# Up-projection of a gated FFN by seven products, with the hidden rows through DRAM

## The chip, the cores and the metric

The kernel runs on one core of a Trainium2 chip. The metric is device time in microseconds (us) of one execution; lower is better. The core has TensorE (PE, with its weight loads PEld), VectorE (DVE), ScalarE (ACT), GpSimd (POOL) and SyncE (SP, which issues most DMAs).

## The reference

One layer of a decoder step for 1024 prompt tokens and 8 x 4 sample tokens (T = 1056 columns in all, D = 1024 features). Latent attention and a state-space branch are merged and projected by w_out; then a gated FFN with a causal width-3 convolution on its up-projection, and an embedding gate, follow. The part that the change touches, in float32:

```python
x = x + mixed @ lw['w_out']
up = rmsnorm(x, lw['g_ffn']) @ lw['w_up']              # 1024 -> 2 x 2816
full = jnp.concatenate([buf, up], axis=1)              # two rows of history in front
conv = lw['conv_b'] + full[:, 0:s] * lw['conv_w'][0]   # + taps 1 and 2
a, v = jnp.split(conv, 2, axis=-1)
x = x + (jax.nn.gelu(a) * v) @ lw['w_down']            # 2816 -> 1024
x = x + jax.nn.sigmoid(rmsnorm(x, lw['g_ple']) @ lw['w_ple_gate']) * (p @ lw['w_ple_proj'])
```

The outputs also include the last rows of the up-projection.

## The kernel before

Features lie on partitions (128 at a time) and tokens on columns. To keep float32 accuracy each operand of a matmul is split into a high part, rounded to float32r by a cast on ACT, and a low part, the rest, by a subtraction on DVE or GpSimd (split, L79). mm3 (L83) then makes three matmuls for each product: high by high, high by low, low by high. The tokens are cut into three blocks of BLK = 352 columns.

The program is written in order and the tile framework places instructions on each engine's queue and adds the semaphores; each engine works its queue in order. Tiles of one tag share a number of buffers (bufs), and a writer waits until the last reader of its buffer is done.

*w_out.* For each of 8 output chunks o, 3 blocks x 8 k x 3 matmuls accumulate in PSUM (tile pm). DVE adds them to the residual x2, which stays in SBUF for all tokens; hi_lo and squares make the operands gh and gl2 of the up-projection and the sums of squares. The norm's factor of each token (rms_sums, rsqrt at L93, rms_rows) is not in the operands: it is multiplied in when the up-projection leaves PSUM (scaled_).

*FFN.* There are 22 hidden blocks of 128 rows (NH), each with a gate half a and a value half v, so 44 up-halves (up_half, L1690). An up-half makes 24 products of 352 columns, which scaled_ takes out of PSUM (L1712). conv (L1721) makes the convolution: a first term on ACT, two taps on DVE with two SBUF operands each (L1726; L1728 for the sample tokens). Then Gelu on ACT, the product of the halves and its split on DVE. The weights of an up-half (up_w, wload) come by one DMA of 512 KB, a cast on ACT and a subtraction on GpSimd (L81). After two hidden blocks down() (L1778) multiplies them with their rows of w_down: for each block and each output chunk two hidden blocks are added up in PSUM, and DVE adds the result to x2 (L1787). The last down() also prepares the operands of the embedding gate.

*Embedding gate.* For each of 8 output chunks and each block: 24 matmuls with w_ple_gate (gate), 6 with w_ple_proj (rest), the sigmoid on ACT, the sum, turned back by TensorE and written out (out_turn).

The order around it is the plain order of the program text: up-halves run one after another, down() of two hidden blocks is traced between two up-halves, and `last_rows` sends out the up-projection's last rows at the end.

## Time and profile before

| | |
|---|---|
| median of 3 runs | 2093.94 us (2093.68 to 2095.9) |
| span of the profiled execution | 2091.9 us |
| PE busy | 2004.0 us (96%), 12558 matmuls |
| PEld busy | 1888.6 us (90%) |
| DVE busy | 1154.0 us (55%) |
| ACT busy | 741.4 us (35%) |
| POOL busy | 552.8 us (26%) |
| granted TensorE clock, mean | 0.974 |
| DMA | 134.58 MB, mean 64 GB/s |

The profiled execution's own time is its span, from the first to the last instruction; the runs' median lies 2.0 us above it. Busy times of PE are of pipelined matmuls, whose recorded durations overlap; the distance of their starts tells their pace. Idle time of an engine that is not the bottleneck costs nothing.

### The profile page before, as it was taken

The page shows a single profiled execution, that of the slowest core. Times are in us where ns is not written, and L with a number is a line of the kernel's source. Part 1 is how long each engine was busy: PE and PEld are TensorE (multiplying, and loading weights), DVE is VectorE, ACT ScalarE, POOL GpSimd, SP SyncE. Part 2 cuts the span into 40 slices and gives each one's busy share as a digit, 9 for nine tenths or more (in the row PEclk, how much of TensorE's full clock was granted, in tenths as well). Part 3 has the DMA queues.
Part 4 walks back from the last instruction along what each step waited for, and adds up shares of the span by engine and source line. Part 5 has one row for each costly group of instructions (what it writes and reads, how often), then busy time and mean ns, then how long its engine had stood idle before and what let it go on. Part 6 is the DMA issues. An engine that isn't in the chain of part 4 may idle for free.

```text
span 2091.9 us, 32712 instructions
## 1 busy us (share of the span) xinstructions
PE 2004.0 (96%) x12558; PEld 1888.6 (90%) x12558; DVE 1154.0 (55%) x2481; ACT 741.4 (35%) x1499; POOL 552.8 (26%) x679
## 2 busy tenths in 40 slices
PE   7998999999998799999999999999999999999999
PEld 6997888888786688889999999999999999999898
DVE  6517532245878856665655555555545554556612
ACT  5522332343665545444333312222221222124422
POOL 1106341111223312223431412222222222214432
PEclk9999999999999979999999999999999999999999
DMA  7402222243321000004441211111111111111121
GB/s 247 125 18 59 61 68 63 66 142 106 91 61 40 28 12 1 2 26 155 129 154 42 71 41 51 51 41 37 56 44 48 31 61 41 51 31 55 45 73 52
DMA packets 175942, 134.58 MB, mean 64 GB/s; under 512 B 34577, under 2 KB 162500, under 8 KB 175786
## 3 DMA queue, kind: packets, MB, share of 16 engines
q1 hardware_dynamic: 168874, 123.84, 19.8%
q10 hardware_dynamic: 6912, 8.65, 1.2%
q8 instruction: 99, 1.62, 0.3%
q14 instruction: 57, 0.47, 0.1%
HBM read 104.87 MB, written 26.24 MB: 63 GB/s over the span
## 4 chain that ended last, share of the span: by engine, by line
PE 80%; DVE 10%; ACT 4%; issue 2%; DMA 2%; POOL 1%; SPq 0%; ACTq 0%; DVEq 0%; POOLq 0%
PE pu L85 9%; PE pu L84 9%; PE pu L86 9%; PE pm L85 5%; PE pm L86 5%; PE pm L84 5%; PE pd L84 4%; PE pd L86 3%; PE pd L85 3%; PE pt L84 3%; PE pt L86 2%; PE pt L85 2%; PE pv L1372 2%; PE p L84 2%; PE p L86 1%
## 5 line engine op out<-in xcount | busy, mean ns | idle before, releaser
L84 PE MATMUL pu<-gh,wh 128*128 128x352 f32 x1248 | 404.8, 324 | 0.0
L86 PE MATMUL pu<-gh,wl 128*128 128x352 f32 x1248 | 404.6, 324 | 0.0
L85 PE MATMUL pu<-gl,wh 128*128 128x352 f32 x1248 | 403.9, 324 | 0.0
L86 PEld LDWEIGHTS pu<-gh,wl 128*128 128x128 f32 x1248 | 235.8, 189 | 0.0
L84 PEld LDWEIGHTS pu<-gh,wh 128*128 128x128 f32 x1248 | 235.7, 189 | 0.1
L85 PEld LDWEIGHTS pu<-gl,wh 128*128 128x128 f32 x1248 | 235.5, 189 | 0.1
L81 POOL TENSOR_TENSOR wl<-ws,wh 128x1024 fp32r<-128x1024 f32 x68 | 167.4, 2462 | 132.3 <-ACT wh L80 126.8
L1726 DVE SCALAR_TENSOR_TENSOR cv<-up,cw,cv 128x1024 f32<-128x1024 f32 (+2 forms) x92 | 157.0, 1707 | 58.2 <-ACT cv L1722 58.1
L1787 DVE TENSOR_TENSOR x<-pd,x 128x352 f32<-128x352 f32 x264 | 135.9, 522 | 92.2 <-PE pd L86 92.2
L84 PE MATMUL pd<-hh,dwh 128*128 128x352 f32 x528 | 172.6, 327 | 7.6 <-DVE x L1787 7.6
L85 PE MATMUL pd<-hl,dwh 128*128 128x352 f32 x528 | 170.4, 323 | 0.0
L86 PE MATMUL pd<-hh,dwl 128*128 128x352 f32 x528 | 170.4, 323 | 0.0
L1712 DVE TENSOR_TENSOR up<-pu,t 128x352 f32<-128x352 f32 x132 | 66.9, 509 | 162.6 <-PE pu L86 162.6
L80 ACT CAST wh<-ws 128x1024 fp32r<-128x1024 f32 x68 | 71.4, 1050 | 168.0 <-PE pu L85 149.5
L86 PE MATMUL pm<-xh,wl 128*128 128x352 f32 x384 | 127.8, 333 | 0.0
L85 PE MATMUL pm<-xl,wh 128*128 128x352 f32 x384 | 127.1, 331 | 0.0
L84 PE MATMUL pm<-xh,wh 128*128 128x352 f32 x384 | 126.8, 330 | 0.0
L84 PEld LDWEIGHTS pd<-hh,dwh 128*128 128x128 f32 x528 | 99.3, 188 | 12.3 <-DVE x L1787 12.3
L85 PEld LDWEIGHTS pd<-hl,dwh 128*128 128x128 f32 x528 | 99.6, 189 | 0.1
L86 PEld LDWEIGHTS pd<-hh,dwl 128*128 128x128 f32 x528 | 99.4, 188 | 0.0
L1372 PEld LDWEIGHTS pv<-Vt,Pt 128*128 128x128 f32 x576 | 78.8, 201 | 3.7 <-ACT Pt L1358 0.5
L1372 PE MATMUL pv<-Vt,Pt 128*128 128x65 f32 x576 | 78.3, 278 | 0.1
(705 smaller groups left out, 4728.5 us busy)
## 6 DMA issues: line engine op xcount, KB each, us to landing
ws<-w_up SPq DMA_DIRECT2D x44, 512.0 KB
wst<-w_in SPq DMA_DIRECT2D x16, 512.0 KB
cb<-cache_ckv SPq DMA_DIRECT2D x64, 128.0 KB
dga<-go ACTq DMA_DIRECT2D x24, 176.0 KB
dgs<-go ACTq DMA_DIRECT2D x24, 176.0 KB
ga<-dga SPq DMA_DIRECT2D x8, 528.0 KB
gs<-dgs SPq DMA_DIRECT2D x8, 528.0 KB
x<-dxt SPq DMA_DIRECT2D x8, 528.0 KB
```

Source lines behind the costliest of these rows:

```text
L80: A.copy(hi, src)
L81: (eng or G).tensor_tensor(lo, src, hi.bitcast(F32), OP.subtract)
L84: PE.matmul(out, lh, rh, start=start, stop=False)
L85: PE.matmul(out, lh, rl, start=False, stop=False)
L86: PE.matmul(out, ll, rh, start=False, stop=stop_)
L1372: PE.matmul(W["pv"][:, j, :DV + 1], Pts[k][:, q0:q0 + 128], Vb[hp][:, k, e], start=k == 0, stop=k == i)
L1712: V.tensor_tensor(U[:, 2 + n * BLK:2 + n * BLK + w], pu[n][:, :w], rbc[:, n * BLK:n * BLK + w], OP.mult)
L1726: V.scalar_tensor_tensor(C[:, c0:c1], U[:, c0 + tp:c1 + tp], w[tp], C[:, c0:c1], op0=OP.mult, op1=OP.add)
L1787: V.tensor_tensor(x2[:, o, c], pd, x2[:, o, c], OP.add)
```

## The change

The up-projection of a hidden block is seen as a 2 x 2 by 2 x 2 block product. The weights' blocks are the two halves of the 1024 features by the two halves a and v; the operand's blocks are the two halves of the features by two quarters (QW = 264 columns) of a token half (HW = 528). Strassen's scheme in Winograd's form makes it with seven products instead of eight. Each product has 4 k x 3 matmuls of 264 columns. The sums of weight blocks and of operand blocks that it needs are made before the split into high and low parts (wprod, operands), the sums of products in PSUM or when they leave it (up_pair). The norm's factor now goes into the operands (scale).

The order of hidden blocks is `occ`: hidden blocks 0 to 3 for the first token half alone, 4 to 21 for both halves, and 0 to 3 again for the second half; so wprod runs 26 times. Weight parts are made three products ahead (ahead). Operands of the second token half are made in steps between the products of the first four (todo), the gate half's convolution, Gelu and the product of the halves in steps of the next occurrence (post).

w_out is made by token halves in blocks of 264 columns, with its weights loaded and split once per half; the residual goes to DRAM (dx2). The merge, which makes w_out's operands, writes them in quarters (mx).

The hidden rows are no longer split and multiplied at once. They go to DRAM (dhid). After all of the up-projection three token blocks (384, 384, 288 columns) are worked one after another (block): hidden rows of the block are loaded and split (hid_in, hid_out), w_down is multiplied with all 22 hidden blocks added up in PSUM, and then the block's embedding gate follows. w_down, w_ple_gate and w_ple_proj are loaded and split once per block (wunit: units of up to 4 x 128 rows, the cast on ACT and the subtraction on GpSimd). The next block's hidden rows are loaded and split during the gate.

```diff
+HW = T // 2
+QW = T // 4
...
-        mh = pm.tile([128, 8, T], F32R, name="mh")
-        ml = pm.tile([128, 8, T], F32R, name="ml")
+        mx = [[[x_tile(pm, 16) for _ in "hl"] for _ in range(2)] for _ in range(4)]
...
+        NJ = 4
+        occ = [(j, 0, 1) for j in range(NJ)] + [(j, 0, 2) for j in range(NJ, NH)] + [(j, 1, 1) for j in range(NJ)]
+        ORDER = (1, 6, 2, 7, 5, 4, 3)
+        def raw_tile():
+            return praw.tile([128, 8, 128], F32, name="raw", tag="raw", bufs=5)
+        raws = {}
...
+        wsum = {}
+        def wprod(i, m):
+            a, v = raws[i]
+            a1, a2, v1, v2 = a[:, 0:4], a[:, 4:8], v[:, 0:4], v[:, 4:8]
+            if m == 6:
+                s = wsum[i] = wp.tile([128, 2, 4, 128], F32, name="wsum", tag="ws", bufs=1)
+                G.tensor_tensor(s[:, 0], v1, v2, OP.add)
+                G.tensor_tensor(s[:, 1], s[:, 0], a1, OP.subtract)
+            if m == 7:
+                G.tensor_tensor(v1, a1, v1, OP.subtract)
+            if m == 3:
+                G.tensor_tensor(a2, a2, wsum[i][:, 1], OP.subtract)
+            s = {1: a1, 2: a2, 4: v2, 7: v1, 3: a2}.get(m)
+            if s is None:
+                s = wsum[i][:, 0 if m == 5 else 1]
+            w = wp.tile([128, 2, 4, 128], F32R, name="wx", tag="w", bufs=4)
+            A.copy(w[:, 0], s)
+            (G if m in (2, 5, 4) else V).tensor_tensor(w[:, 1], s, w[:, 0].bitcast(F32), OP.subtract)
+            if m == ORDER[-1]:
+                load_raw(i + 2)
+            return w
+        wseq = [lambda i=i, m=m: wprod(i, m) for i in range(len(occ)) for m in ORDER]
+        wq = []
+        def ahead(n):
+            while wseq and len(wq) < n:
+                wq.append(wseq.pop(0)())
...
+        def wo_evac(h, o, p_):
+            x = XP[h, o % 4][:, o // 4]
+            x_q = x.rearrange("p (n c) -> p n c", n=2)
+            V.tensor_tensor(x_q, p_[:, :, :QW], x_q, OP.add)
+            SP.dma_start(dx2[o * 128:(o + 1) * 128, h * HW:(h + 1) * HW], x)
             if o == 0:
-                A.activation(sqs[:, c], x2[:, o, c], AF.Square, scale=1.0 / 32.0)
+                A.activation(sqs, x, AF.Square, scale=1.0 / 32.0)
             else:
-                A.activation(sq, x2[:, o, c], AF.Square, scale=1.0 / 32.0)
-                eng.tensor_tensor(sqs[:, c], sqs[:, c], sq, OP.add)
...
+            def hl(m, k, src, eng):
+                hi, lo = (x[:, k] for x in tile_of(m))
+                A.copy(hi, src)
+                eng.tensor_tensor(lo, src, hi.bitcast(F32), OP.subtract)
+            def scale(k):
+                for g in range(2):
+                    x = XP[h, k][:, g]
+                    V.scalar_tensor_tensor(x, x, gcol["g_ffn"][:, 4 * g + k:4 * g + k + 1], rbh, op0=OP.mult, op1=OP.mult)
+            def first(k):
+                b11, b12, b21, b22 = (XP[h, k][:, g, q * QW:(q + 1) * QW] for g in range(2) for q in range(2))
+                hl(1, k, b11, V)
+                hl(2, k, b21, G)
+                hl(3, k, b22, V)
+                V.tensor_tensor(b11, b12, b11, OP.subtract)
+                G.tensor_tensor(b12, b22, b12, OP.subtract)
+            def second(k):
+                t1, t3, b21, b22 = (XP[h, k][:, g, q * QW:(q + 1) * QW] for g in range(2) for q in range(2))
+                V.tensor_tensor(b22, b22, t1, OP.subtract)
+                hl(6, k, b22, V)
+                hl(7, k, t3, G)
+                hl(5, k, t1, V)
+                G.tensor_tensor(b21, b21, b22, OP.subtract)
+                hl(4, k, b21, V)
+            return ([lambda k=k: scale(k) for k in range(4)] + [lambda k=k: first(k) for k in range(4)] +
+                    [lambda k=k: second(k) for k in range(4)])
+        for h in range(2):
+            for o in range(8):
+                wh, wl = W.pop(0)
+                if o < 7:
+                    W.append(wload((w_out[:, :, (o + 1) * 128:(o + 2) * 128], 0, 8)))
+                elif h == 0:
+                    W.append(wload((w_out[:, :, 0:128], 0, 8)))
+                else:
+                    ahead(2)
+                p_ = psq_.tile([128, 2, 512], F32, name="q")
+                for n in range(2):
+                    for k in range(8):
+                        mh, ml = mx[2 * h + n][k // 4]
+                        mm3(p_[:, n, :QW], wh[:, k], wl[:, k], mh[:, k % 4], ml[:, k % 4], k == 0, k == 7)
+                if h and o == 0:
+                    rst = half_sums()
+                wo_evac(h, o, p_)
+                if h == 0 and o < 4:
+                    x_load(1, o)
+                if h == 0 and o == 7:
+                    todo = operands(0)
+                if h and o == 1:
+                    half_rows(rst)
+                if h and o > 1:
+                    for _ in range(2):
+                        todo.pop(0)()
+                if h and o in (3, 5):
+                    load_raw((o - 3) // 2)
...
+            def prods(m, t, start):
+                w = wq.pop(0)
+                ahead(3)
+                for n in range(ng):
+                    xh_, xl_ = XT[g0 + n][m]
+                    for k in range(4):
+                        o_ = t[:, n, :QW]
+                        for x, (l_, r_) in enumerate(((w[:, 0, k], xh_[:, k]), (w[:, 0, k], xl_[:, k]), (w[:, 1, k], xh_[:, k]))):
+                            PE.matmul(o_, l_, r_, start=start and k + x == 0, stop=k + x == 5, skip_group_check=not start)
...
+            P = acc()
+            prods(1, P, True)
+            v = P[:, :ng, :QW]
+            A.copy(part(1, 0), v)
+            step()
+            Q = acc()
+            prods(6, Q, True)
+            V.tensor_tensor(part(0, 1), Q[:, :ng, :QW], part(1, 0), OP.add)
+            step()
+            prods(2, P, False)
+            A.copy(part(0, 0), v)
+            step()
+            prods(7, Q, False)
+            V.tensor_tensor(part(1, 1), Q[:, :ng, :QW], part(1, 0), OP.add)
+            step()
+            R = acc()
+            prods(5, R, True)
+            V.tensor_tensor(part(1, 1), R[:, :ng, :QW], part(1, 1), OP.add)
+            step()
+            prods(4, Q, False)
+            V.tensor_tensor(part(1, 0), Q[:, :ng, :QW], part(1, 0), OP.add)
...
+            conv(1)
+            prods(3, R, False)
+            V.tensor_tensor(part(0, 1), R[:, :ng, :QW], part(0, 1), OP.add)
+            def hidden():
+                V.tensor_tensor(Cs[0][:, :tot], Cs[0][:, :tot], Cs[1][:, :tot], OP.mult)
+                SP.dma_start(dhid[j * 128:(j + 1) * 128, g0 * HW:g0 * HW + tot], Cs[0][:, :tot])
+            post.append(lambda: conv(0))
+            post.append(lambda: A.activation(Cs[0][:, :tot], Cs[0][:, :tot], AF.Gelu_apprx_tanh))
+            post.append(hidden)
...
+        def hid_split(b, r, t, eng):
+            pool, n_ = (hid1, 16) if r < 8 else (p2, 6)
+            w = TB[b][1]
+            hi, lo = (pool.tile([128, 2, 384], F32R, name="hd", tag="hd", bufs=n_)[:, :, :w] for _ in "hl")
+            split(t, hi, lo, eng)
+            hp_[r] = hi, lo
+        def wunit(x):
+            kind, b, o, kg = units[x]
+            t = unit_raw(units[x])
+            if x + 2 < len(units):
+                unit_raw(units[x + 2])
+            n = 2 if (kind == "d" and kg == 5) or (kind == "g" and kg == 2) else 4
+            s = t[:, 4 * (kg % 2):4 * (kg % 2) + n]
+            w = wp.tile([128, 2, 4, 128], F32R, name="wx", tag="w", bufs=4)
+            split(s, w[:, 0, :n], w[:, 1, :n])
+            return w
+        wseq += [lambda x=x: wunit(x) for x in range(len(units))]
...
+            def down_group(pd, kg):
+                wt = wq.pop(0)
+                ahead(3)
+                for k in range(4 * kg, min(4 * kg + 4, NH)):
+                    hi, lo = (x[:, k % 2] for x in hp_[k // 2])
+                    mm3(pd, wt[:, 0, k % 4], wt[:, 1, k % 4], hi, lo, k == 0, k == NH - 1)
+            def down_out(o, pd):
+                V.tensor_tensor(xb[o], pd, xb[o], OP.add)
+                gg = GG[o] = pA.tile([128, 2, HW + 4], F32R, name="gg", tag="A", bufs=8)[:, :, :w]
+                g = gcol["g_ple"][:, o:o + 1]
+                A.activation(gg[:, 0], xb[o], AF.Copy, scale=g)
+                V.scalar_tensor_tensor(gg[:, 1], xb[o], g, gg[:, 0].bitcast(F32), op0=OP.mult, op1=OP.subtract)
+                if o == 0:
+                    A.activation(sqb, xb[o], AF.Square, scale=1.0 / 32.0)
+                else:
+                    sq = p2.tile([128, 384], F32, name="sq", bufs=2)[:, :w]
+                    A.activation(sq, xb[o], AF.Square, scale=1.0 / 32.0)
+                    (V if o == 7 else G).tensor_tensor(sqb, sqb, sq, OP.add)
...
+            nxt = list(range(NP_)) if b < 2 else []
+            for o in range(8):
+                pg_ = gate(o)
+                if o == 0:
+                    rst = sums()
+                pp_ = proj(o)
+                if o == 0:
+                    rows(rst)
+                rest(o, pg_, pp_)
+                if o:
+                    out_turn(o - 1)
+                for r in list(hraw):
+                    hid_out(*r)
+                for r in nxt[:2]:
+                    hid_in(b + 1, r)
+                nxt = nxt[2:]
```

## Rows read from the trace of the kernel before

**Rows 1.** Windows: us; busy PE, PEld, DVE, ACT, POOL (instructions); clock, DMA share, GB/s.

```profile
1068.70:1161.00 92.30, 92.30 (x580) 92.30 (x578) 49.28 (x70) 30.62 (x56) 19.56 (x8) 1.00 0.28 93
1162.00:1948.00 786.00, 777.11 (x4807) 770.28 (x4807) 443.46 (x705) 207.14 (x257) 206.39 (x260) 1.00 0.15 47
1948.00:2091.90 143.90, 135.74 (x847) 131.35 (x845) 42.64 (x82) 37.10 (x71) 39.34 (x32) 0.96 0.21 61
```

**Rows 2.** Timeline of TensorE: first matmul of a down() call, start and duration.

```profile
1299.69 0.43 PE L84 MATMUL pd<-hh,dwh 128*128 128x352 f32 x1 [0.58 <-DVE x L1787]
```

**Rows 3.** Timeline of TensorE: dense runs of 384, 288, 256 columns, first and last.

```profile
56.20 0.34 PE L84 MATMUL pm<-wah,xh 128*128 128x384 f32 x1
...
60.22 0.34 PE L86 MATMUL pm<-wah,xl 128*128 128x384 f32 x1
60.40 0.30 PE L84 MATMUL pm<-wah,xh 128*128 128x288 f32 x1
...
63.44 0.30 PE L86 MATMUL pm<-wah,xl 128*128 128x288 f32 x1
...
594.09 0.28 PE L85 MATMUL pt<-wkl,ch 128*128 128x256 f32 x1
...
594.57 0.28 PE L86 MATMUL pt<-wkh,cl__5571 128*128 128x256 f32 x1
```

**Rows 4.** Groups of GpSimd by shape: count, busy us and mean ns, idle before.

```profile
L81 POOL TENSOR_TENSOR wl<-ws,wh 128x1024 fp32r<-128x1024 f32 x57 | 138.2, 2424 | 108.4 <-ACT wh L80 102.9
...
L1896 POOL TENSOR_TENSOR y<-y,x 128x352 f32<-128x352 f32 x21 | 19.7, 942 | 47.5 <-DVE y L1895 47.5
...
L81 POOL TENSOR_TENSOR wkl<-kst,wkh 128x512 fp32r<-128x512 f32 x4 | 5.1, 1279 | 1.0 <-ACT wkh L80 1.0
```

**Rows 5.** Groups of DVE by shape, same columns.

```profile
L1787 DVE TENSOR_TENSOR x<-pd,x 128x352 f32<-128x352 f32 x264 | 135.9, 522 | 92.2 <-PE pd L86 92.2
...
L1759 DVE TENSOR_TENSOR cv<-cv 128x1056 f32<-128x1056 f32 x21 | 26.1, 1242 | 0.0
...
L81 DVE TENSOR_TENSOR wal<-wast,wah 128x512 fp32r<-128x512 f32 x4 | 2.8, 688 | 0.4 <-ACT wah L80 0.4
...
L1726 DVE SCALAR_TENSOR_TENSOR cv<-up,cw,cv 128x352 f32<-128x352 f32 x4 | 2.3, 585 | 1.5 <-ACT cv L1722 1.4
```

**Rows 6.** Timelines of DVE and GpSimd at three places of the FFN.

```profile
1181.82 1.27 DVE L1726 SCALAR_TENSOR_TENSOR cv<-up,cw,cv 128x1024 f32<-128x1024 f32 x1
1181.91 3.44 POOL L81 TENSOR_TENSOR wl<-ws,wh 128x1024 fp32r<-128x1024 f32 x1
...
1223.65 2.41 POOL L81 TENSOR_TENSOR wl<-ws,wh 128x1024 fp32r<-128x1024 f32 x1
1224.57 0.53 DVE L1787 TENSOR_TENSOR x<-pd,x 128x352 f32<-128x352 f32 x1 [0.44 <-PE pd L86]
...
1259.26 2.41 POOL L81 TENSOR_TENSOR wl<-ws,wh 128x1024 fp32r<-128x1024 f32 x1
1260.43 2.32 DVE L1726 SCALAR_TENSOR_TENSOR cv<-up,cw,cv 128x1024 f32<-128x1024 f32 x1 [1.59 <-ACT cv L1722]
1262.67 0.24 DVE L1728 SCALAR_TENSOR_TENSOR cv<-up,cw,cv 128x32 f32<-128x32 f32 x1
1262.84 1.27 DVE L1726 SCALAR_TENSOR_TENSOR cv<-up,cw,cv 128x1024 f32<-128x1024 f32 x1
```

**Rows 7.** Groups of ACT by shape, same columns.

```profile
L1722 ACT ACTIVATE cv<-up,cw 128x1024 f32<-128x1024 f32 x43 | 53.2, 1238 | 0.0
...
L80 ACT CAST wah<-wast 128x512 fp32r<-128x512 f32 x8 | 5.0, 624 | 0.8 <-DMA wast<-w_in 0.8
```

**Rows 8.** Timeline of DVE: first and last step of an inverse root.

```profile
1166.88 0.17 DVE L1651 TENSOR_SCALAR msx<-pt 128x8 f32<-128x8 f32 x1 [1.22 <-PE pt L1647]
...
1169.19 0.17 DVE L111 SCALAR_TENSOR_TENSOR rst<-rf_a,rf_i 128x9 f32<-128x9 f32 x1
```

**Rows 9.** The page's 40 equal slices: what DMA moved.

```profile
GB/s 247 125 18 59 61 68 63 66 142 106 91 61 40 28 12 1 2 26 155 129 154 42 71 41 51 51 41 37 56 44 48 31 61 41 51 31 55 45 73 52
```

More of the change, by code (lines that the diff above doesn't have):

```diff
@@ L1614, in body @@
         mo.close()
[L1617 to L1624 removed]
+        praw = ctx.enter_context(tpool(name="praw", bufs=1, side="right"))
@@ new lines, in body, with operands, tile_of @@
+        XT = {}
+        def operands(h):
+            pool, n_ = (px, 12) if h == 0 else (pm, 16)
+            X = XT[h] = {}
+            def tile_of(m):
+                if m not in X:
+                    p_, b_ = (px, 12) if h == 0 and len(X) < 6 else (pm, 16)
+                    X[m] = x_tile(p_, b_), x_tile(p_, b_)
+                return X[m]
+            def hl(m, k, src, eng):
+                hi, lo = (x[:, k] for x in tile_of(m))
+                A.copy(hi, src)
+                eng.tensor_tensor(lo, src, hi.bitcast(F32), OP.subtract)
+            def scale(k):
+                for g in range(2):
+                    x = XP[h, k][:, g]
[17 more added lines that the diff above has]
+                    [lambda k=k: second(k) for k in range(4)])
@@ new lines, in body @@
+        todo = []
+        for k in range(4):
+            x_load(0, k)
+        for h in range(2):
[26 more added lines that the diff above has]
+                    load_raw((o - 3) // 2)
@@ new lines, in body @@
+        R2 = {}
+        todo = [lambda: R2.update(r=half_sums()), lambda: half_rows(R2["r"])] + operands(1)
+        for i in range(NH):
+            up_pair(i)
+            if i == NJ - 1:
+                assert not todo
+        pX.close()
+        TB = ((0, 384), (384, 384), (768, 288))
+        NP_ = NH // 2
+        w_dn = I["w_down"].rearrange("o (k p) n -> p (o k) n", p=128)
+        w_pp = I["w_ple_proj"].rearrange("o (k p) n -> p (o k) n", p=128)
+        dhv = dhid.rearrange("(k p) t -> p k t", p=128)
@@ new lines, in body, with unit_raw @@
+        units = []
+        for b in range(3):
+            units += [("d", b, o, kg) for o in range(8) for kg in range(6)]
+            units += [("g", b, o, kg) for o in range(8) for kg in range(3)]
+        rawq, wraw = {}, [0]
+        def unit_raw(u):
+            kind, b, o, kg = u
+            key = kind, b, o, kg // 2
+            if key not in rawq:
+                t = rawq[key] = raw_tile()
+                oc = slice(o * 128, (o + 1) * 128)
+                if kind == "d":
+                    k0, k1 = 8 * (kg // 2), min(8 * (kg // 2) + 8, NH)
+                    SP.dma_start(t[:, :k1 - k0], w_dn[:, k0:k1, oc])
+                elif kg < 2:
+                    SP.dma_start(t, w_pg[:, :, oc])
+                else:
+                    SP.dma_start(t[:, :2], w_pp[:, :, oc])
+            return rawq[key]
@@ new lines, in body, with hid_in, hid_out, none @@
+        hraw = {}
+        def hid_in(b, r):
+            hraw[b, r] = hid_load(b, r)
+        def hid_out(b, r):
+            hid_split(b, r, hraw.pop((b, r)), V)
+        def none():
+            pass
+        for r in range(0, 8, 2):
+            todo += [lambda r=r: hid_in(0, r), none, lambda r=r: (hid_out(0, r), hid_in(0, r + 1)), none,
+                     lambda r=r: hid_out(0, r + 1)]
+        for i in range(NH, len(occ)):
+            up_pair(i)
+        while post:
+            step()
@@ L1806, in last_rows @@
                 PE.transpose(pt[:18, j * 128:(j + 1) * 128], LU[:, q + j], ident)
-            lo_ = pn2.tile([18, 512], F32, name="lo_", bufs=LOB)
+            lo_ = p2.tile([18, 512], F32, name="lo_", bufs=1)
             A.copy(lo_, pt[:18])
-            SP.dma_start(cvp[:, q * 128:(q + 4) * 128], lo_[0:2])
-            SP.dma_start(cvs[:, q * 128:(q + 4) * 128], lo_[2:18])
-        ready = [q for q in range(0, NH2, 4) if max(order.index(q + i) for i in range(4)) < NH2 - 2]
-        for q in ready:
-            last_rows(q)
+            A.dma_start(cvp[:, q * 128:(q + 4) * 128], lo_[0:2])
@@ L1830, in p_turn @@
+        def p_turn(b):
+            w, ld = TB[b][1], pld.pop(b)
+            pT[b] = [p2.tile([128, 2, 384], F32R, name="pT" + x, bufs=1) for x in "hl"]
             for k in range(2):
                 pt = ps.tile([128, 512], F32, name="pt")
-                for j in range(nj):
-                    PE.transpose(pt[:, j * 128:j * 128 + n], ld[:n, j, k * 128:(k + 1) * 128], ident[:n, :n])
-                c, w = slice(j0 * 128, j0 * 128 + nj * n), nj * n
-                A.copy(pTh[k][:, c], pt[:, :w])
@@ L1836, in p_turn @@
-                V.tensor_tensor(pTl[k][:, c], pt[:, :w], pTh[k][:, c].bitcast(F32), OP.subtract)
-        sqs3 = pn2.tile([128, T], F32, name="sqs3", tag="hl", bufs=3)
-        def after(o, c):
-            hi_lo(o, c, gcol["g_ple"][:, o:o + 1])
-            squares(o, c, sqs3, pn2.tile([128, S + 2 + NB * 6], F32, name="sq3", tag="up")[:, :BLK], G)
-        down((NH - 2, NH - 1), after)
-        for n in range(3):
-            p_turn(n)
-        w_pp = I["w_ple_proj"].rearrange("o k n -> (o k) n")
@@ L1919, in host_consts @@
+        for r in range(8, NP_):
+            hid_in(0, r)
+        for r in range(8, NP_):
+            hid_out(0, r)
+        for b in range(3):
+            block(b)
 def host_consts():
```

429 lines of the change are left out of this document (209 added, 220 removed).

## The prediction

> **What bounds the kernel now.** I read the work by stage first. From the w_out projection on, TensorE is busy nearly throughout: the projection 92.3 of 92.3 us, the FFN 777 of 786, the gate stage 136 of 144 [rows 1]. VectorE (DVE) is at 56% of the FFN and GpSimd (POOL) at 26%. So the time is TensorE's, and a change gains what it takes off TensorE and loses what it makes TensorE wait. One regular wait exists already: TensorE sits 0.58 us before the first matmul of each of the ten inner down() calls [rows 2].
>
> The pace of matmuls comes next, since a recorded duration overlaps its neighbours and only starts tell it. The projection's 576 products of 352 columns fill 92.3 us: 0.1602 us each [rows 1]. Of 384 columns, 24 start in 56.20 to 60.22, 0.1748 each; of 288, 24 in 60.40 to 63.44, 0.1322; of 256, five in 594.09 to 594.57, 0.120 [rows 3].
>
> Last I looked at how DVE and GpSimd get on, because the change loads both. In each up-half the first convolution tap on DVE takes 2.32 us where the second takes 1.27. It started at 1260.43 while GpSimd's split ran from 1259.26 to 1261.67, and ended 1.08 us after it: it waited [rows 6]. In the other order GpSimd waits: its split at 1181.91 took 3.44 us, ending 2.26 us after a tap that started before it, where 2.41 is usual [rows 6]. An add that reads one operand from PSUM is not held up: 0.53 us inside a GpSimd split [rows 6]. So DVE work with both operands in SBUF and GpSimd work add up; about 0.19 us of a DVE operation and 0.15 of a GpSimd one still overlap.
>
> The Trainium skill states this (SBUF — State Buffer, "Who interferes with whom"): a DVE instruction with two SBUF inputs and a GpSimd instruction that reads SBUF exclude each other for the whole instruction. The rows agree, with 1.05 us lost per first tap, but for the short overlap. By the rule to the letter the shared work of part 3 would take its full durations, 92 + 70 us in place of the 77 + 63 that I take, and the kernel 2149 us.
>
> **1. Columns on TensorE.** 264 columns: the line through 288 and 384 gives 0.1322 - 24 x 0.000444 = 0.1215, the row at 256 plus 8 columns 0.1236; I take 0.122. Up-projection: 44 x 24 x 3 = 3168 x 0.1602 = 507.5 becomes 22 pairs x 2 halves x 7 products x 12 = 3696 x 0.122 = 450.9: -56.6 (-58 to -51). w_out: 576 x 0.1602 = 92.3 becomes 768 x 0.122 = 93.7: +1.4. Down, gate and embedding: 2304 x 0.1602 = 369.1 becomes 768 x (0.1748 + 0.1748 + 0.1322) = 370.0: +0.9. Together **-54**.
>
> **2. Prices on the other engines.** GpSimd, 512 columns 1.28, 352 columns 0.94, so 264 cost 0.76 and 1024 cost 2.41 [rows 4]. DVE, two SBUF operands: 512 0.69, 1056 1.24, so 264 0.44 and 768 0.95; a tap of 352 0.59 and of 1024 1.27, so 528 0.76 [rows 5, 6]. DVE from PSUM: 352 0.52 [rows 5], so 528 0.70. ACT: a cast of 512 0.62, a first tap of 1024 1.24 [rows 7].
>
> wprod puts seven 512-column operations on GpSimd per occurrence (four sums, three low parts): 9.0 us, of which 7 x (1.28 - 0.15) = 7.9 exclude DVE. On DVE it puts four low parts, 2.8 us (2.0 exclusive); the four taps, with 0.24 for a tap's sample columns [rows 6] left aside, cost 5.1 (4.3) at full width and 3.1 (2.3) at half width, the product of the halves 1.2 (1.0) or 0.7 (0.5).
>
> **3. The eight half-width occurrences** (the first four hidden blocks, once per token half). TensorE needs 84 x 0.122 = 10.25 us. The shared work is 7.9 + 2.0 + 2.3 + 0.5 = 12.7 us if every overlap is used, 15.5 by full durations. That already exceeds TensorE.
> The first four also carry operands(1): per k four GpSimd operations of 264 (3.0 us, 2.4 exclusive), two scalings (1.5, 1.1) and seven DVE operations of 264 (3.1, 1.8); over four k 21 exclusive, 30 full. Four occurrences: 4 x 12.7 + 21 = 72, or 4 x 15.5 + 30 = 92, against 41. Both queues hold ready work, so I take 77, near the low end: **+36** (+31 to +51).
> The last four carry eight splits of hidden rows, 768 columns on DVE each: 6 exclusive, 7.6 full: 57 to 70, and the casts wait for the row's DMA on ACT. I take 63: **+22** (+16 to +29).
>
> **4. The eighteen full-width occurrences.** TensorE 168 x 0.122 = 20.5 us, shared work 7.9 + 2.0 + 4.3 + 1.0 = 15.3: it fits. But the chain is in order. After product 4, DVE adds (0.70), ACT makes conv(1)'s first term (1.24), DVE its taps and their sample columns (3.0), then the add that empties product 3 (0.70), then ACT and DVE the same for conv(0) (4.3), queued ahead of the add that empties the next 6. These 9.9 us end about 11.0 after product 4 with the hand-overs; product 7 needs it 3 products after 4 plus one, at 4 x 2.93 = 11.7. Unhindered it just fits. Each of four taps meets GpSimd (9 of 20.5 us busy) and loses up to 1.05; two hits cost 2.1, of which 0.7 is slack. I take 1.2 us per occurrence: **+22** (0 to +45, that is 2.5 each). Queued behind the late add are product 7, and behind that every later product.
>
> **5. w_out's second half.** From o = 2 operands(0) runs beside the weights' split and the squares: per o 2.26 + 1.16 + 21/6 = 6.9 us exclusive against 48 x 0.122 = 5.9. Six o's: **+6** (0 to +9); late next is the first occurrence's product 6.
>
> **6. Stalls removed.** The ten waits before down() go (0.58 with 0.16 of a matmul's start: 7.4), and with them the per-tile work of the last down(), where GpSimd sums squares: I take **-12** (-16 to -8).
>
> **7. The last stage in three blocks.** Down per o: 66 x 0.1748 = 11.5 us; GpSimd 5.5 x 1.28 + 1.0 = 8.0; hidden by TensorE, and in the third block 66 x 0.1322 = 8.7 against 7.8, still hidden. The inverse root of each block took from 1166.88 to 1169.36 before [rows 8], under two gate passes; now only one embedding pass of 6 x 0.1748 = 1.05 stands between: 3 x 1.6 = +5. In the gate passes of blocks 0 and 1 GpSimd's 3.7 and the next rows' low parts and sums 1.5 make 5.2 exclusive of TensorE's 30 x 0.1748 = 5.24, and DMA moves 0.79 + 0.64 + 0.20 MB per pass, 311 GB/s, where the busiest slice shows 247 [rows 9]: +4 (0 to +16). Third block: GpSimd 4.1 against 3.97: +1. Hand-over from up to down, where rows 16 to 21 are loaded and split: +3 (0 to +6). Together **+13** (+5 to +28).
>
> The moved DMAs: hidden rows are written and read back by SP, behind weight loads that wait for one of five raw tiles; this is hidden in the full-width part (0.5 MB per 20.5 us), and is in the terms of the last four and of the gate passes elsewhere.
>
> Sum: -54 + 36 + 22 + 22 + 6 - 12 + 13 = +33. On the profiled span of 2091.9 that is 2125; the median of the runs is 2.0 above the span, so **2127 us**.
>
> **Rivals.**
> A, the other sign: in the half-width occurrences DVE and GpSimd overlap, and each engine alone is the limit. GpSimd's own time is 9.0, some 9.6 with its small copies, per occurrence and 12 for operands(1): 50 against 41, +9; the last four, with more copies, 11 against 10.25, +3; without blocking the chain of part 4 costs nothing, w_out nothing, and part 7 10. -54 + 9 + 3 - 12 + 10 = -44: 2050. For it: GpSimd and DVE are both under 60% busy on average [rows 1]. Against: the 2.32 us taps [rows 6]. Between A and the forecast it decides at what the half-width occurrences cost beyond TensorE: the forecast has 58 us, and below 58 - 33 = 25 us in all (3 each) the kernel is faster. A partial overlap therefore lands at 2060 to 2095.
> B: the full-width chain is hit by GpSimd at all four taps, 2.9 to 3 us per occurrence: 54 in place of 22, 2158.
> C: the gate passes are bound by DMA at 247 GB/s: 1.63 MB take 6.6 us, +1.36 x 6 x 2 = 16 in place of 4: 2139. For it: no slice moves more.
> D: the change doesn't do what it says, since 264 columns go no faster than 288: 3696 x 0.1322 = 489 gains 19 only: 2165. Against: 0.120 at 256 [rows 3].
>
> **Chances.** Forecast 0.38, within 2105 to 2155. A and its partial forms 0.36, of which 0.06 end within 0.2% (4.2 us, about what a measurement of this kernel can tell from no change) and 0.30 below. B 0.15, C 0.08, D 0.03, all slower. So faster 0.30, same 0.06, slower 0.64. All low ends together give 2074, all high ends 2199; the range 2058 to 2172 leaves about 0.1 out on each side.
>
> **What would show it.** Starts of 264-column products 0.122 apart, where nothing waits. TensorE's idle time ended by DVE's adds and by GpSimd's or DVE's weight parts, in the first four occurrences (some 77 us) and last four (63), against 20.5 to 23 us for each full-width one; DVE's taps and low parts well above 0.76 and 0.69. About 1.6 us idle at each block's inverse root. Wrong: half-width occurrences at 10 to 12 us, or a last stage that waits on DMA for tens of us.

## The result and the profile after

The changed kernel takes **2156.5 us** (median of 4 runs, 2150.0 to 2159.6) against 2093.8 of the kernel before, measured beside it: ratio 1.0281 [1.0257, 1.0306], 63 us slower. The prediction was 2127 us in a range of 2058 to 2172, slower with 0.64. The direction and the range hold; the loss is about twice the one forecast, just beyond the 2105 to 2155 that I had given the forecast itself, and one stage alone lies 37 us above its forecast.

First the windows by stage, columns as in [rows 1]: merge, w_out, the first four half-width occurrences, the eighteen full-width ones, the last four, the hand-over (3.3 us, left out here), and the last stage in blocks.

```profile
975.60:1074.00 98.40, 98.40 (x627) 96.88 (x626) 55.31 (x87) 34.65 (x64) 42.95 (x38) 0.98 0.39 114
1074.00:1210.70 136.70, 110.01 (x784) 105.43 (x783) 52.72 (x75) 35.49 (x62) 71.07 (x48) 0.90 0.41 131
1210.70:1293.50 82.80, 55.66 (x354) 52.20 (x353) 75.68 (x104) 37.31 (x77) 64.33 (x61) 0.79 0.23 71
1293.50:1665.60 372.10, 372.10 (x3027) 370.27 (x3026) 296.66 (x323) 168.92 (x253) 296.60 (x304) 1.00 0.25 77
1665.60:1735.80 70.20, 53.35 (x338) 49.31 (x336) 61.62 (x75) 34.88 (x62) 57.91 (x64) 0.85 0.40 121
...
1739.10:2153.80 414.70, 397.10 (x2465) 390.50 (x2465) 115.51 (x180) 188.43 (x361) 296.94 (x255) 0.98 0.55 161
```

The span grew from 2091.9 to 2153.8 us, by 61.9. Up to the end of the merge 5.3 of it arose: 4.1 ahead of the merge, in code that did not change (the profiles of this case's eleven kernels begin the merge anywhere between 970.9 and 980.3), and 1.2 in the merge itself, which now writes quarters. The w_out stage went from 92.3 us [rows 1] to 136.7: **+44.4**. FFN and gate stage together, with the few us around them, went from 930.9 to 943.1: +12.2. The columns were saved as forecast, but a stage that the change seemed to touch lightly lost more than all the rest together.

In w_out TensorE waits for a single buffer, `ws`: each chunk is loaded into it, cast and split, and only then can the next load start. I call this chain the ring. Rows of the timeline for the path of a weight chunk (start, duration, engine; L1136 loads 512 KB into `ws`, L82 casts it, L83 makes the low half):

```profile
1094.47 2.35 POOL L83 TENSOR_TENSOR wl<-ws,wh 128x1024 fp32r<-128x1024 f32 x1 [4.62 <-PE q L88]
1096.84 0.38 SPq L1136 DMA_DIRECT2D ws<-w_out  x1
1096.87 0.19 PEld L88 LDWEIGHTS q<-X,wl 128*128 128x128 f32 x1 [2.13 <-POOL wl L83]
1101.42 1.05 ACT L82 CAST wh<-ws 128x1024 fp32r<-128x1024 f32 x1 [5.54 <-DMA ws<-w_out]
1102.55 2.38 POOL L83 TENSOR_TENSOR wl<-ws,wh 128x1024 fp32r<-128x1024 f32 x1 [4.45 <-ACT wh L82]
1104.95 0.38 SPq L1136 DMA_DIRECT2D ws<-w_out  x1
1104.98 0.19 PEld L88 LDWEIGHTS q<-X,wl 128*128 128x128 f32 x1 [0.71 <-POOL wl L83]
```

The next load is issued only when the low half is done (1096.84 behind 1094.47 + 2.35), lands 4.6 us later, is cast in 1.05 and split in 2.38: from one load to the next 8.1 us. The matmuls of a chunk now need 48 x 0.122 = 5.9 us, because each chunk is loaded twice, once per token half; before, a chunk had 72 products of 0.160 [rows 1], 11.5 us, and covered the ring.

Groups by shape in two of the three parts of the up-projection: taps, weight parts and operand splits on DVE, sums on GpSimd (count, busy us and mean ns, idle before). The first fence is of the eighteen full-width occurrences, the second of the first four.

```profile
L1839 PE MATMUL q<-X,wx 128*128 128x264 f32 x3027 | 372.6, 285 | 0.0
L1890 DVE SCALAR_TENSOR_TENSOR cv<-up,cw,cv 128x1024 f32<-128x1024 f32 x69 | 112.9, 1636 | 23.7 <-ACT cv L1881 23.7
L1674 DVE TENSOR_TENSOR wx<-raw,wx 128x512 fp32r<-128x512 f32 x54 | 61.1, 1131 | 6.9 <-ACT wx L1673 6.9
L1666 POOL TENSOR_TENSOR raw<-raw 128x512 f32<-128x512 f32 x18 | 40.5, 2252 | 0.0
```

```profile
L1839 PE MATMUL q<-X,wx 128*128 128x264 f32 x337 | 54.1, 326 | 22.8 <-ACT wx L1673 10.5 <-DVE up L1862 5.9 <-DVE up L1856 3.6
L1748 DVE TENSOR_TENSOR X<-xp,X 128x264 fp32r<-128x264 f32 x20 | 15.9, 833 | 1.1 <-ACT X L1747 1.1
L1674 DVE TENSOR_TENSOR wx<-raw,wx 128x512 fp32r<-128x512 f32 x12 | 12.9, 1072 | 0.8 <-ACT wx L1673 0.8
```

A split of 512 columns on DVE takes 1.1 us where it took 0.69 [rows 5], a tap of 1024 takes 1.64 where 1.27 is unhindered [rows 6], and the GpSimd sum of L1666 2.25 where 1.28 was usual for 512 columns [rows 4]. These operations take longer in both parts; but of these two only the half-width occurrences show idle time of TensorE (22.8 us against 0.0).

### The profile page after: what moved, and what is told of

Same layout as the page of the kernel before. It is cut to its first block, busy times and chain, and to the rows that moved or that the text cites. A ratio compares the mean times of both kernels' runs of the same rounds, so it can differ in the third digit from the quotient of the medians.

```text
span 2153.8 us, 35915 instructions
## 1 busy us (share of the span) xinstructions
PE 1987.4 (92%) x13281; PEld 1862.9 (86%) x13281; DVE 1217.2 (57%) x2386; ACT 933.9 (43%) x1940; POOL 1077.4 (50%) x1119
## 4 chain that ended last, share of the span: by engine, by line
PE 71%; DVE 11%; DMA 6%; POOL 5%; ACT 4%; issue 3%; SPq 1%; ACTq 0%; POOLq 0%; DVEq 0%
PE q L1839 19%; PE pd L86 4%; PE pd L87 4%; PE pd L88 4%; PE pm L87 4%; PE pm L88 4%; PE pm L86 4%; PE pt L86 2%; PE pv L1376 2%; DMA ws<-w_out 2%; PE pt L88 2%; PE pt L87 2%; POOL wl L83 2%; PE p L86 1%; PE p L88 1%
## 5 line engine op out<-in xcount | busy, mean ns | idle before, releaser
L1839 PE MATMUL q<-X,wx 128*128 128x264 f32 x3696 | 479.5, 292 | 39.7 <-ACT wx L1673 14.4
L1839 PEld LDWEIGHTS q<-X,wx 128*128 128x128 f32 x3696 | 470.3, 195 | 48.3 <-ACT wx L1673 19.9
L83 POOL TENSOR_TENSOR wx<-raw,wx 128x512 fp32r<-128x512 f32 (+1 forms) x216 | 258.4, 1207 | 112.7 <-ACT wx L82 111.3
L82 ACT CAST wx<-raw 128x512 fp32r<-128x512 f32 (+1 forms) x216 | 123.3, 572 | 190.6 <-PE pd L88 134.0
L86 PE MATMUL pd<-hd,wx 128*128 128x384 f32 (+1 forms) x528 | 171.4, 325 | 3.1 <-ACT wx L82 3.1
L87 PE MATMUL pd<-hd,wx 128*128 128x384 f32 (+1 forms) x528 | 170.5, 323 | 0.0
L88 PE MATMUL pd<-hd,wx 128*128 128x384 f32 (+1 forms) x528 | 170.4, 323 | 0.0
L1673 ACT CAST wx<-raw 128x512 fp32r<-128x512 f32 x130 | 80.2, 617 | 93.2 <-PE q L1839 59.2
L86 PEld LDWEIGHTS pd<-hd,wx 128*128 128x128 f32 x528 | 99.6, 189 | 3.4 <-ACT hd L82 3.3
L88 PEld LDWEIGHTS pd<-hd,wx 128*128 128x128 f32 x528 | 99.7, 189 | 0.0
L87 PEld LDWEIGHTS pd<-hd,wx 128*128 128x128 f32 x528 | 99.6, 189 | 0.0
L83 POOL TENSOR_TENSOR wl<-ws,wh 128x1024 fp32r<-128x1024 f32 x24 | 58.8, 2450 | 74.7 <-ACT wh L82 63.5
L88 PE MATMUL q<-X,wl 128*128 128x264 f32 x256 | 78.2, 306 | 18.1 <-POOL wl L83 18.1
L83 POOL TENSOR_TENSOR wl<-wst,wh 128x1024 fp32r<-128x1024 f32 x16 | 39.3, 2455 | 102.7 <-ACT wh L82 98.6
L1674 DVE TENSOR_TENSOR wx<-raw,wx 128x512 fp32r<-128x512 f32 x78 | 85.7, 1099 | 7.7 <-ACT wx L1673 7.7
```

What stands on the lines that cost most here:

```text
L82: A.copy(hi, src)
L83: (eng or G).tensor_tensor(lo, src, hi.bitcast(F32), OP.subtract)
L86: PE.matmul(out, lh, rh, start=start, stop=False)
L87: PE.matmul(out, lh, rl, start=False, stop=False)
L88: PE.matmul(out, ll, rh, start=False, stop=stop_)
L1673: A.copy(w[:, 0], s)
```

## The experiments

**One weight buffer.** The w_out chunks are loaded three chunks ahead of their use into the tiles of the raw up-weights (`wo_load`), and split from there (`wo_split`). In this and the following cuts the lines are shortened and the comments are mine.

```diff
-    W.append(wload((w_out[:, :, (o + 1) * 128:(o + 2) * 128], 0, 8)))
+    W.append(wo_split(8 * h + o + 1))   # cast on ACT, low half on GpSimd, from its own raw tile
+    wo_load(8 * h + o + 3)              # SP: next DMA
```

> The changed kernel, with w_out's weight chunks loaded three chunks ahead into the raw tiles instead of into one buffer (ws) that is refilled after its split. Theory of the ring: load, cast and split of one chunk follow each other in one buffer, about 8.3 us per chunk where the half-width matmuls of a chunk need 5.9; with the loads ahead the w_out stage falls from 136.7 us to 98 to 108 us and the kernel to about 2118 to 2128 us. Theory of the shared work of DVE and GpSimd: the stage is long because the operands of the first token half are made beside it; then only its first half gets shorter, the stage stays above 120 us and the kernel above 2140 us.

Measured: 2127.0 us, ratio to before 1.0124 [1.0096, 1.0152], 29.5 less than the changed kernel. The kernel before took 2098.6 us beside this run and 2093.8 beside the changed kernel, so a difference of medians of two experiments is uncertain by some 5 us (by the ratios this one is 33); the windows of the stages are safer. Here w_out, and the up-projection with the hand-over:

```profile
1077.30:1187.90 110.60, 99.64 (x786) 98.47 (x785) 60.27 (x75) 35.34 (x62) 71.66 (x48) 0.94 0.50 155
1187.90:1715.10 527.20, 479.59 (x3714) 469.93 (x3712) 436.48 (x507) 244.79 (x395) 420.14 (x428) 0.95 0.27 83
```

The w_out stage fell by 26.1 us, the other stages stayed. Thirteen of the 16 chunks now take 5.8 to 6.8 us, against five; three of the second half still take 10.6 to 11.0 (beside operands(0)). The ring is the cause of most of the stage's loss, 26.1 of 44.4 us.

**GpSimd that only writes.** In the half-width occurrences, and in the operands of the second token half, GpSimd's reads are replaced by writes: this kernel leaves out these sums and low parts.

```diff
-    G.tensor_tensor(s[:, 0], v1, v2, OP.add)
+    only_write(s[:, 0])                 # three G.memset of the same tile
```

> Leaves out part of the computation: in the eight half-width occurrences and for the second token half's operands, each GpSimd sum or low part is replaced by three GpSimd memsets of the same tile, so GpSimd is as busy (about 1.4 us per tile of 512 columns) but reads no SBUF. Theory of exclusion (GpSimd's reads and DVE's two-operand work add up): the first four occurrences fall from 82.8 us to 55 to 65 and the last four from 70.2 us to 45 to 55, the kernel to about 2110 to 2125 us. Rival (GpSimd's own time and the order of the queues set the pace, the engines do not exclude each other): both groups stay within 5 us of what they were and the kernel within 2150 to 2160 us. The w_out stage stays as it was by both.

Measured: 2115.3 us in a single execution, span 2113.5. The first four took 58.6 us instead of 82.8, and the last four with the hand-over 57.6 instead of 73.5 (without it 55.8 instead of 70.2, just above the 45 to 55 expected); w_out stayed, at 138. The window of the first four, the same group of operand splits as above (its line number has moved), and what GpSimd did instead:

```profile
1211.60:1270.20 58.60, 47.05 (x354) 44.50 (x353) 49.81 (x104) 37.00 (x77) 55.34 (x140) 0.94 0.33 100
...
L1769 DVE TENSOR_TENSOR X<-xp,X 128x264 fp32r<-128x264 f32 x20 | 8.0, 430 | 2.6 <-ACT X L1765 2.5
L1659 POOL MEMSET wx<- 128x512 f32 x36 | 18.8, 526 | 0.5
```

A split on DVE takes 0.43 us instead of 0.83, though GpSimd is busy for 55.3 of these 58.6 us (three memsets of 512 columns take 1.58 us, where I had expected 1.4). It is GpSimd's reading that held DVE up, not GpSimd being busy. (Of the two groups' 40 us this is the most that can be put down to it: a write does not have to wait for ACT's cast either, for which GpSimd's low parts waited 11.9 us in the first four of the changed kernel.) The Trainium skill says so (SBUF — State Buffer, "Who interferes with whom"): a DVE instruction with two SBUF inputs is in conflict with a GpSimd instruction that reads SBUF, and not with one that only writes; these rows agree, 0.83 against 0.43 us.

**The sums on VectorE.** The four sums of a weight's products go to DVE in the half-width occurrences (`E = V if occ[i][2] == 1 else G`).

> The changed kernel with the four sums of weight blocks made on DVE instead of GpSimd in the eight half-width occurrences. Theory of exclusion: four operations of 1.28 us become four of 0.69 in the shared sum, 12.7 us per occurrence becomes 10.2 at best, so the two groups lose 2 to 4 us per occurrence: the first four 66 to 75 us, the last four 55 to 62, the kernel about 2130 to 2142 us. Rival (DVE's queue alone is the limit there): DVE gets 2.8 us more per occurrence and the groups grow by 10 to 22 us together, the kernel 2165 to 2180 us.

Measured: 2138.4 us, ratio 1.0192 [1.0157, 1.0226], 18 less than the changed kernel. The kernel is where it was expected by exclusion, but neither group is. The last four with the hand-over fell by 9.6 us to 63.9, expected at 55 to 62; the first four, expected at 66 to 75, fell only by 4.3:

```profile
1211.50:1290.00 78.50, 58.94 (x353) 55.67 (x352) 74.57 (x118) 38.16 (x77) 46.51 (x48) 0.77 0.25 75
...
1662.50:1726.40 63.90, 48.12 (x338) 43.53 (x337) 60.65 (x90) 34.88 (x63) 37.02 (x52) 0.97 0.42 128
```

DVE is busy 74.6 of 78.5 us there. Moving the work from GpSimd shortens it (a sum of 512 takes 0.68 on DVE where nothing holds it up), but in the first four DVE is then nearly full, with operands(1) on it. That is its recorded time, which still contains waiting: its operand splits average 0.70 us there, against 0.43 beside writes. So it is not shown that DVE's own work is the limit.

**No half-width occurrences.** All 22 pairs at full width; operands(1) are made in one piece ahead of the pairs, the first block's hidden rows are split inside its first down pass.

```diff
-        NJ = 4
+        NJ = 0
+        while todo:
+            todo.pop(0)()               # operands(1)
```

> The changed kernel without half-width occurrences: all 22 hidden blocks at full width, the second token half's operands made before the first of them (TensorE waits for them), and the first token block's hidden rows loaded and split within its first pass of the down-projection. Theory of the shared work (weight parts are the same work per occurrence whether TensorE has 10.25 or 20.5 us for it): the up-projection takes 22 x 20.7 = 455 us, plus 20 to 30 us for the operands and 5 to 10 us at the hand-over, in place of 528: the kernel falls by 30 to 45 us to about 2112 to 2127 us. Rival (the half-width occurrences cost their operands and row splits, not their weight parts): the same work only moves to where TensorE waits for it, and the kernel stays within 10 us of 2156 us.

Measured: 2124.1 us, ratio 1.0122 [1.0096, 1.0148], 32.4 less than the changed kernel. Windows of the first pair, of the other 21, and of the last stage:

```profile
1207.50:1260.80 53.30, 34.44 (x186) 30.34 (x185) 38.88 (x65) 17.87 (x41) 29.89 (x31) 0.68 0.12 35
1260.80:1697.70 436.90, 435.31 (x3531) 431.08 (x3529) 350.09 (x379) 201.34 (x298) 346.23 (x354) 1.00 0.25 79
1697.70:2118.50 420.80, 396.90 (x2465) 388.24 (x2465) 123.94 (x188) 195.66 (x369) 295.47 (x255) 0.98 0.57 167
```

The first pair takes 32.5 us longer than the others: TensorE is idle for 18.9 and slow for the rest, at a granted clock of 0.68. And yet the up-projection with the hand-over takes 38 us less (490.2 against 528.4; the hand-over is now part of the last stage), of which the last stage gives 6 back. The half-width occurrences were meant to hide operands(1); they cost more than what they hide, since each repeats the weights' whole shared work for half the columns. (The edit also moves the splits of the first block's hidden rows into its first down pass; the two parts were not run apart.)

**Both together.** The edits of the first and the fourth experiment.

> The w_out chunks loaded ahead and all 22 pairs at full width, together. If the ring of the weight chunk and the half-width occurrences are two separate losses, their gains add: 2156.5 - 29.5 - 32.4 = 2095 us (2089 to 2101), with a w_out stage near 111 us and an up-projection near 490 us. If they are one loss seen twice (GpSimd's and VectorE's shared work, which only moves), the two together give no more than the better one alone, 2115 to 2125 us.

Measured: 2094.1 us, ratio 0.9996 [0.9983, 1.0008]: no difference from the kernel before.

```profile
1073.40:1184.30 110.90, 100.99 (x785) 100.02 (x784) 58.66 (x75) 35.18 (x62) 71.61 (x48) 0.94 0.50 155
1184.30:1237.50 53.20, 34.41 (x186) 30.33 (x184) 38.77 (x65) 17.83 (x41) 29.85 (x31) 0.68 0.12 36
1237.50:1674.30 436.80, 435.21 (x3531) 431.08 (x3529) 350.23 (x379) 200.97 (x298) 346.18 (x354) 1.00 0.25 79
```

The w_out stage of 110.9 us and the up-projection of 490.0 are those of the two single edits (110.6 and 490.2), so the gains add: these are two separate losses, and together they are the whole loss of the change. That the median is within 1 us of the 2095 expected is closer than medians of different experiments can be trusted.

**The rest of the shared work on VectorE.**

```diff
-            split(wo_raw.pop(x), wh, wl)
+            split(wo_raw.pop(x), wh, wl, V if x > 10 else G)
...
-                hl(2, k, b21, G)
+                hl(2, k, b21, V)        # and each other step of operands(h) that was G's
...
+            # h == 1: scale, then the operands of product 1, 6, 2; those of 7, 5, 4 inside the first pair
```

> On top of both: in the second half of w_out and in the first pair's operands, every elementwise step that reads two SBUF operands goes to VectorE (the low halves of the last five w_out chunks, the sums of squares, GpSimd's eight operand splits and eight differences of each half), and the second half's operands come in the order of the products that use them, four of the products' operands inside the first pair. The exclusion theory: VectorE's own time is some 38 us in the 35 us of w_out's last six chunks, against 58 us of taking turns, so the w_out stage falls from 111 to 98 to 103 us; the first pair falls from 53 to 36 to 42 us; the kernel 2066 to 2078 us. The rival, that it is the amount of VectorE's work and not the taking of turns: VectorE has more to do now, the w_out stage stays at 108 to 115 us, the first pair gains 5 us at most by the order, and the kernel is at 2088 to 2098 us.

Measured: 2071.9 us, ratio 0.9901 [0.9881, 0.9921]. The w_out stage is 98.6 us, as the exclusion theory had it; GpSimd's busy time there fell from 71.6 to 36.5 us and DVE's did not rise (58.7 to 55.0), though DVE took over the work. The edit also starts operands(0) one output chunk earlier; what that gives by itself was not run. The first pair takes 45.7, between the two forecasts (36 to 42, or 48 and more). Windows of the w_out stage, and of the first pair in three stretches:

```profile
1071.10:1169.70 98.60, 96.48 (x786) 95.81 (x785) 55.04 (x101) 35.26 (x62) 36.48 (x21) 1.00 0.56 174
...
1174.00:1185.60 11.60, 3.79 (x20) 2.81 (x20) 8.73 (x26) 2.26 (x7) 0.00 (x0) 0.63 0.17 47
1185.60:1194.00 8.40, 7.68 (x32) 7.17 (x32) 8.40 (x25) 5.55 (x17) 4.04 (x1) 0.50 0.00 0
1194.00:1203.00 9.00, 5.31 (x29) 5.00 (x28) 2.69 (x8) 2.17 (x7) 7.13 (x4) 0.80 0.00 0
```

What is left there is the inverse root and the scaling, 11.6 us in which TensorE has next to nothing, and then 8.4 us at a granted clock of 0.50. In the third stretch one of GpSimd's weight parts is late, beside a row of DVE's splits (timeline of both and of TensorE):

```profile
1189.96 7.39 POOL L1674 TENSOR_TENSOR wx<-wsum,wx 128x512 fp32r<-128x512 f32 x1 [16.55 <-ACT wx L1673]
...
1193.74 2.49 DVE L1748 TENSOR_TENSOR X<-xp,X 128x264 fp32r<-128x264 f32 x7
...
1197.40 5.22 PE L1874 MATMUL q<-X,wx 128*128 128x264 f32 x28 [3.31 <-POOL wx L1674]
```

**The last stage.** The rows of a block's inverse root go to TensorE after the second gate chunk, and the output's transposes run two chunks behind (tile `y` has a fourth buffer for it); once by itself on the changed kernel, once on top of the last kernel.

```diff
-                if o == 0:
-                    rows(rst)
+                if o == 1:
+                    rows(rst)           # and rest(0) behind it
...
-                if o:
-                    out_turn(o - 1)
+                if o > 1:
+                    out_turn(o - 2)
```

> The same edit of the last stage, by itself on the changed kernel. Term 7's reading (idle time of TensorE at each block's inverse root, and the chain of an output chunk one chunk behind): the last stage falls from 414.7 us by 8 to 12 us, and the kernel to 2144 to 2149 us. Rival (the wait moves on to the split weights): 2153 to 2157 us.

> On top of that: in the last stage the rows of the inverse root are taken to TensorE after the second gate chunk instead of behind the first, and the output's transposes run two chunks behind instead of one. The three idle times at the inverse root (2.6, 2.3 and 1.9 us) go, and the five idle times before output transposes (6.8 us) for the most part: 8 to 12 us less than the run before it. If the last stage is bound by the split weights of the gate instead, the idle time moves to the next wait and the time falls by under 3 us.

Measured alone: 2144.9 us, ratio to before 1.0245 [1.0230, 1.0259]; the last stage fell from 414.7 to 404.6 us, within 8 to 12. The timeline of TensorE at the first block's inverse root, changed kernel and this one (first matmul, and what it waited for):

```profile
1848.53 0.51 PE L2113 MATMUL pt<-ident,rst 128*128 128x128 f32 x3 [2.28 <-DVE msx L2103]
```

```profile
1842.06 0.51 PE L2113 MATMUL pt<-ident,rst 128*128 128x128 f32 x3 [0.73 <-DVE msx L2103]
```

On top of the others: 2071.2 us, ratio to before 0.9881 [0.9866, 0.9896]. The last stage fell by 5.4 us (420.9 to 415.5), less than 8 to 12, and the kernel by 0.7, which the spread does not tell from nothing: its profile begins the merge 4.2 us later. Part of the idle time did move to the next wait, as the rival had it: TensorE's waits for inverse roots and transposes fell from 13.0 to 2.4 us, but those ended by GpSimd's weight parts rose from 1.0 to 4.9. This kernel and the one before it beat both kernels of the case, by 1.2 and 1.0% of the kernel before.

**The first pair's weight parts on VectorE.** On top of all of it, `G if m in (2, 5, 4) else V` becomes `G if m in (2, 5, 4) and i else V`.

> On top of the kernel with all edits: the low halves of the first pair's weight parts that GpSimd made (products 2, 5 and 4) go to VectorE. In the run before, one of them took 7.39 us on GpSimd beside a dense row of VectorE's splits, and TensorE waited 3.3 us for it. If GpSimd was kept from its turn by that row, the part on VectorE comes in its place in the row and takes 0.7 us: the 3.3 us shrink to 1 or 2, the first pair falls from 45.7 to 42.5 to 44.5 us, and the kernel by 1 to 3 us to 2068 to 2070. If VectorE is simply full there, its row ends 2 us later and the first pair stays at 45 to 47 us.

Measured: 2067.2 us, ratio to before 0.9861 [0.9844, 0.9877], the lowest median of the case. The first pair fell from 45.7 to 43.8 us, and the wait for this weight part from 3.31 to 1.43:

```profile
1194.30 0.68 DVE L1674 TENSOR_TENSOR wx<-wsum,wx 128x512 fp32r<-128x512 f32 x1
...
1195.04 3.19 PE L1874 MATMUL q<-X,wx 128*128 128x264 f32 x24 [1.43 <-DVE wx L1674]
```

Both are what was expected if GpSimd had been kept from its turn, and not if DVE were simply full (45 to 47 us). The kernel fell by 4.0 us (2071.2 to 2067.2), a little more than the 1 to 3 expected; the pair accounts for 1.9, and the rest is within the spread of such runs.

## Why the prediction came out as it did

**Part 1 (columns) was right.** Starts of 264-column products lie 0.122 us apart in the median, and a full-width occurrence takes 20.67 us with all its overheads: rival D falls.

**Part 3 (half-width occurrences) was right in its mechanism and 13 us low.** 77 and 63 us were forecast, 82.8 and 70.2 measured: the first four in the middle of their bounds (72 to 92), the last four at the top of theirs (57 to 70). For the first four I chose near the low end because "both queues hold ready work"; that was too low. The granted clock was 0.79 and 0.85 in these stretches, which the sum did not have; what it cost is not shown. With GpSimd's reads gone the same occurrences took 58.6 and 55.8, so exclusion is up to some 40 us of the two. The time by full durations, 92 and 70, fits the last four and not the first. Rival A, where the two engines overlap, falls; half-width occurrences at 14 to 15 us even without the conflict are also more than A's 11 to 12.5.

**Part 4 (full-width chain) was 19 us high.** Forecast 1.2 us per occurrence, measured 0.17 (20.67 against 20.5). The hits came: the taps average 1.64 us and not 1.27, and sample taps were hit too. But the chain just had the room. Rows of DVE's timeline in one occurrence (sample taps of conv(1), product 4's add, conv(1)'s first tap, product 3's add, conv(1)'s second tap, a tap that was hit, a sample tap that was hit, the add that frees product 7), and below them ACT's first term of conv(0):

```profile
1331.02 0.54 DVE L1892 SCALAR_TENSOR_TENSOR cv<-ub,cw,cv 128x32 f32<-128x32 f32 x2 [0.55 <-ACT cv L1888]
1331.94 0.71 DVE L1869 TENSOR_TENSOR up<-q,up 128x528 f32<-128x528 f32 x1 [0.38 <-PE q L1839]
1333.96 1.29 DVE L1890 SCALAR_TENSOR_TENSOR cv<-up,cw,cv 128x1024 f32<-128x1024 f32 x1 [1.31 <-ACT cv L1881]
1335.16 0.70 DVE L1901 TENSOR_TENSOR up<-q,up 128x528 f32<-128x528 f32 x1
1335.78 1.70 DVE L1890 SCALAR_TENSOR_TENSOR cv<-up,cw,cv 128x1024 f32<-128x1024 f32 x1
...
1339.37 2.31 DVE L1890 SCALAR_TENSOR_TENSOR cv<-up,cw,cv 128x1024 f32<-128x1024 f32 x1
1341.61 1.27 DVE L1892 SCALAR_TENSOR_TENSOR cv<-ub,cw,cv 128x32 f32<-128x32 f32 x1
1342.80 0.69 DVE L1856 TENSOR_TENSOR up<-q,up 128x528 f32<-128x528 f32 x1
...
1335.90 1.25 ACT L1881 ACTIVATE cv<-up,cw 128x1024 f32<-128x1024 f32 x1 [0.35 <-DVE up L1901]
```

From product 4's add to the end of the last one it is 11.55 us, inside the 11.7 that I gave as the room, with the hits in it. My 11.0 without hits was too long, although it left out the last add itself (0.7): the sample taps of conv(1), which I had put on the chain, ran ahead of product 4's add, and product 3's add came between conv(1)'s taps, so that ACT's first term of conv(0) ran under the second tap. Rival B had the same flaw. That the chain fits is close to luck: in each of the seventeen that another full-width one follows, the last add ends only 0.05 to 0.06 us before TensorE starts product 7, with 0.17 us between starts there in place of 0.12, so by these rows a further hit of 1 us would have reached TensorE every time. The total, 2156.5 us, is near rival B's 2158, but not by B's mechanism.

**Part 5 (w_out's second half) is the step that failed.** "+6" measured 136.7 - 93.7 = +43; the two halves of the stage took 62 and 75 us, so that the first half, where operands(0) do not run yet, lost 15 us too. I priced the work of GpSimd and DVE by output chunk and took the weights' way through one `ws` tile as before, although each chunk is now used for half as many columns. The split (2.26 us in my sum, of 2.42 [rows 4]) stood there as work, not as one link of a ring with the load (4.6 us) and the cast (1.05) that each chunk goes through alone; 5.9 us of matmuls no longer cover the 8.1. The first experiment gave 26 us of w_out back; what remained, 17 us, arose beside operands(0), whose exclusion I had seen and sized at 6; the sixth experiment, with this work on DVE, gave 12 of it back, and the last 5 are not explained. The Trainium skill's general advice (Trainium Kernel Development and Optimization, "Best Practices") is to double-buffer so that DMA overlaps compute; this stage had a single buffer, and loads ahead into several gave 26 us of it back.

**Parts 6 and 7 (waits removed, last stage) were right to 8 us** as a sum; no run tells them apart. The sum left 425.6 us for the hand-over and the last stage, which took 418.0. Two of the three idle times at the inverse roots were larger than 1.6 (waits of 2.28, 1.98 and 1.58 us), and TensorE also waited for the output's transposes, which the sum did not have; the one edit of both gave 10 us. Rival C did not happen, though it was near: in the gate passes of blocks 0 and 1 DMA moved 228 and 205 GB/s, and none of TensorE's waits in the last stage was ended directly by a DMA.

So 37 us too little in w_out, 13 too little in the half-width occurrences, 19 too much in the full-width ones, 8 too much behind them, and 5 up to the end of the merge: 2125 + 28 = 2153, the span measured. Misses of 55 us one way and 27 the other partly cancel, so that the total stayed in the range owes something to luck.

What is not settled: how much of the half-width occurrences' remaining 14 us each, without the conflict, is the clock and how much the chain of casts on ACT; no kernel separated them.

## What to carry to other kernels

A change that halves the matmul time behind each loaded weight chunk must be checked against the whole ring of the buffer (DMA, cast, split, release), not against the busy time of any engine: with one buffer the ring is the price per chunk. Splitting a loop to hide preparation repeats the work that is done per weight, so compare what it repeats with what it hides: here 32 us of waiting in the open were cheaper than eight half-width occurrences. Work that DVE and GpSimd take turns on is shortened by giving it to the faster of the two as long as that one is not full.

## What the runs showed of the hardware

The clock fell with the waits and stayed low for a while after them. In the sixth experiment TensorE was busy 3.8 of 11.6 us (1174.0 to 1185.6), and in the next 8.4 us, with 7.7 busy, it was granted 0.50, the lower level of 1.2 GHz: 32 products in 7.7 us, 0.24 each in place of 0.122. These products took 3.8 us longer than at the full clock, and no part of my sum had that. Whether the kernel did is not shown: DVE was busy for all of these 8.4 us, and TensorE then waited 3.31 us for the weight part all the same.

A GpSimd operation among a dense row of DVE's splits can be held up for several of them: a weight part of 1.3 us took 7.39 from 1189.96 on, while DVE ran operand splits and differences of 0.43 us one after another, and ended 1.1 us after that row. So here the engine with the row of short instructions kept its turn. When the same part was put into DVE's own row, it took 0.68.
